# Eight filling tiles, later conditioning columns, a reordered last round with early outputs, a third raw pair, and operand sums in place

## The chip, the core and the metric

The kernel runs on one core of one Trainium2 chip. The metric is the device time of one execution, in microseconds (us). TensorE is called PE, VectorE DVE, ScalarE ACT, GpSimd POOL and SyncE SP in the profile; SP issues all of the kernel's transfers, in one queue.

## What is computed

One decoder block on 1024 tokens of width 1024, in float32. Only the second half of it is touched here:

```python
cond = silu(c) @ ada_w + ada_b            # six vectors: shift1, scale1, gate1, shift2, scale2, gate2
x = x + gate1 * (y @ w_out)               # after the token mixers
h2 = modulate(rmsnorm(x, norm2_g), shift2, scale2)
g_ff, up_ff = split(h2 @ w_ffn_in, 2)     # 1024 -> 2 x 2816
x = x + gate2 * ((silu(g_ff) * up_ff) @ w_ffn_out)
return modulate(rmsnorm(x, norm_f_g), shift_f, scale_f)
```

## The kernel before

Everything is held transposed: features on the 128 partitions, tokens along the free axis, in two halves of 512. `xs[0]` to `xs[7]` are the eight feature tiles of x (`x_76` to `x_83` in the listings). A float32 product is made from three matmuls of split operands (high times high, low times high, high times low). A split is an ACT copy to a rounded high part and a subtraction for the low part (`split`, lines 501 to 503), on DVE or POOL.

The FFN's input projection is done in 22 tiles of 128 gate and 128 up features. A tile is a two-by-two block product by Strassen and Winograd's scheme: seven products, numbered 1 to 7, instead of eight, each of 12 matmuls with 512 columns. Its weights (two raw tiles of 512 KB from `wf`) are combined on DVE into sums (`s_f`, `raw_f`) and split into `w_f_1` to `w_f_7`; the operands of h2 are combined and split once, into `h_p_5`, `h_p_6` and so on for p from 0 to 3. Bank B takes products 1, 6, 7 and 4 in turn with snapshots between, bank C 5 and 3, bank A 2.

Products 1 and 2 need only the first half of the tokens. For some tiles they are made ahead (`ahead_quad`), written to device memory (`ahead`) and read back later. `N_AHEAD` = 12 of these run beside the convolution. `N_FILL` = 4 more, f from 12 to 15, are written in the code between the second half's output projection and the FFN. The other 6 tiles are whole: all seven products inside the loop. `tile_order` spreads the whole tiles over the loop, at places 0, 4, 8, 13, 17 and 21; the partial ones have 60 matmuls, the whole ones 84.

After each pair of tiles, `finish_tile` combines the activations and writes seven operands to device memory (`acts`). It keeps its tiles in two sets of six halves of `xs`, whose own values wait in device memory (`x_mid`) meanwhile. The last 24 conditioning columns (gate2 and the final shift and scale) are a background list: `ada_cols` loads a column block into `xs[5]` or `xs[6]` and reduces it on DVE (line 143), one for each tile begun. Raw weights have four buffers (`N_RAW`), split weights eight (`N_W`).

The down projection follows in three rounds of 4, 4 and 3 pairs. Each round loads the operands, splits them (`fa`), and runs four groups n of seven products; each product is added into `xs` by a gated DVE operation (line 769). In the last round the squares of the finished tiles are summed over features by small matmuls with a vector of ones (line 801). At the end, for three pieces of the tokens (512, 256, 256), a root, a reciprocal and small matmuls (line 851) give the scale, and eight outputs a piece follow on DVE (line 855), ACT (line 857) and SP (line 858).

A scheduler that simulates the engines' times fixes the order of instructions on each engine when the kernel is built; the code's order, waits and priorities bound it. Each engine then runs its own queue in order.

Of the kernel before, what the change touches and what calls it, by code (L numbers as in the profile page):

```python
# [7 lines left out]
F32 = mybir.dt.float32  # L8
# [5 lines left out]
P = 128  # L14
S = 1024
# [18 lines left out]
N_FILL = 4  # L34
# [27 lines left out]
def block_kernel(ctx: ExitStack, tc: tile.TileContext, xT, c, ada, cols, vbias, bs, wsp,  # L62
# [442 lines left out]
    def product(bank, w_units, movs, first, cols=slice(0, H)):  # L505
        n = len(movs)
        for p, ((shi, slo), mv) in enumerate(zip(w_units, movs)):
            mhi, mlo = full(mv)
            for i, (s, m) in enumerate(((shi, mhi), (slo, mhi), (shi, mlo))):
                PE.matmul(bank[:, cols], s, m[:, cols], start=first and p == 0 and i == 0,  # L510
                          stop=p == n - 1 and i == 2, skip_group_check=True)
# [78 lines left out]
    def stationary(name, srcs, width):  # L590

        raw = []
        for i, src in enumerate(srcs):
            r = sb.tile([P, 2, width], F32, tag="raw", name=f"raw_{name}_{i}", bufs=N_RAW)
            nc.sync.dma_start(r, src)
            raw.append(r)
# [6 lines left out]
        def put(*products):  # L603
            for m in products:
# [8 lines left out]
                w = sb.tile([P, 2, H], F32R, tag="w", name=f"w_{name}_{m}", bufs=N_W)[:, :, 0:width]  # L613
# [10 lines left out]
    for p in range(4):  # L624
# [8 lines left out]
        def put(m, src):  # L633
            res[m] = moving_tile(m, f"h2_{p}_{m}")
            split(res[m], src, V)
# [13 lines left out]
    sets = [[xs[k][:, hs(half)] for k in ks for half in range(2)] for ks in ((7, 3, 2), (0, 4, 1))]  # L649
# [7 lines left out]
    def finish_tile(i, g0, g1):  # L657
# [12 lines left out]
        G.tensor_tensor(b12, g1, b12, op=ALU.subtract)  # L670
        moved(i, 7, b12)
        G.tensor_tensor(b11, b12, b11, op=ALU.add)
# [11 lines left out]

    def begin(f):
        st, put = stationary(f"f{f}", [wf[2 * f + 1].rearrange("p (a b) -> p a b", a=2),
                                       wf[2 * f].rearrange("p (a b) -> p a b", a=2)], H)
# [15 lines left out]
    for i, f in enumerate(order):  # L703
# [27 lines left out]
        if full7:  # L731
            A.activation(g0, b_bank, AF.Silu)
        else:
            V.tensor_tensor(g0, b_bank, s1, op=ALU.add)
            A.activation(g0, g0, AF.Silu)  # L735
# [10 lines left out]
    A.activation(warm, epst, AF.Sqrt)  # L746


    for k in (0, 4, 1, 5, 6, 2, 3, 7):
        nc.sync.dma_start(xs[k], x_mid[k])  # L750
    f0 = 0
    for r, pairs in enumerate(ROUNDS):
# [11 lines left out]
        st, banks = {}, {}  # L764

        def gate(bank, dests, cols=slice(0, H)):
            for k, half in dests:
                part = slice(half * H + cols.start, half * H + cols.stop)
                V.scalar_tensor_tensor(xs[k][:, part], bank[:, cols], ccol(GATE2, k),  # L769
                                       xs[k][:, part], op0=ALU.mult, op1=ALU.add)  # L770

        def step(n, m, bank, first, dests):
            product(bank, st[n][m], [v[m] for v in mov], first)
            gate(bank, dests)

        def begin_out(n):
            st[n], put = stationary(f"d{r}_{n}", [src_w[base + i].rearrange("p (a b) -> p a b", a=2)
                                                  for i in (n, n + 4)], pairs * P)
            put(1, 5, 6, 2, 7, 4, 3)
            banks[n] = mm_bank(f"B{r}_{n}")  # L780
            step(n, 1, banks[n], True, ((n, 0),))

        begin_out(0)
        for n in range(4):
            c_bank = cv_bank(f"C{r}_{n}")
            a_bank = gn_bank(f"A{r}_{n}")
            if last_round and n == 0:
                pieces = [(nrm_bank("ssq_nf0"), slice(0, H)),
                          (gn_bank("ssq_nf1"), slice(H, H + 256)),
                          (mm_bank("ssq_nf2"), slice(H + 256, S))]  # L790
                seen = [0, 0, 0]

            def square(i, k):

                bank, part = pieces[i]
                size = part.stop - part.start
                nq = size // P
                t = ev(f"sq_nf{i}_{k}")[:, 0:size]
                A.activation(t, xs[k][:, part], AF.Square)
                for q in range(nq):  # L800
                    PE.matmul(bank[q * 32:(q + 1) * 32, 0:P], ones.broadcast_to([P, 32]),  # L801
                              t[:, q * P:(q + 1) * P], start=seen[i] == 0, stop=seen[i] == KD - 1)
                seen[i] += 1

            fin = last_round and n == 3
            if not fin:
                step(n, 5, c_bank, True, ((n + 4, 1),))
            step(n, 6, banks[n], False, ((n, 1),))
            step(n, 2, a_bank, True, ((n, 0),))
            if last_round:  # L810
                square(0, n)
            if not fin:
                step(n, 7, banks[n], False, ((n + 4, 1),))
            if last_round and not fin:
                square(1, n + 4)
                square(2, n + 4)
            if n < 3:
                begin_out(n + 1)
            if fin:
                step(n, 5, c_bank, True, ((n + 4, 1),))  # L820
                step(n, 7, banks[n], False, ((n + 4, 1),))
# [112 lines left out]
```

## Time and profile before

| | |
|---|---|
| median of 3 runs | 1080.92 us (1079.58 to 1084.81) |
| profiled execution | 1082.03 us, span 1080.2 us |
| PE busy | 996.0 us, 92% |
| DVE busy | 856.5 us, 79% |
| ACT busy | 471.0 us, 44% |
| POOL busy | 379.6 us, 35% |
| data moved | 177.62 MB, mean 164 GB/s |

The span runs from the first to the last instruction. In the sliced view each digit is the busy share, in tenths, of one of 40 equal slices of 27 us; PEclk is the clock that was granted to TensorE. In a list of groups, the part after the bar gives total busy time, the mean duration in ns, and the idle time of the engine just before with what ended it. In a list of waits the three numbers are total us, times and the longest.

### The profile page before, as it was taken

The page shows a single profiled execution, that of the slowest core. Times are in us where ns is not written, and L with a number is a line of the kernel's source. Part 1 is how long each engine was busy: PE and PEld are TensorE (multiplying, and loading weights), DVE is VectorE, ACT ScalarE, POOL GpSimd, SP SyncE. Part 2 cuts the span into 40 slices and gives each one's busy share as a digit, 9 for nine tenths or more (in the row PEclk, how much of TensorE's full clock was granted, in tenths as well). Part 3 has the DMA queues.
Part 4 walks back from the last instruction along what each step waited for, and adds up shares of the span by engine and source line. Part 5 has one row for each costly group of instructions (what it writes and reads, how often), then busy time and mean ns, then how long its engine had stood idle before and what let it go on. Part 6 is the DMA issues. An engine that isn't in the chain of part 4 may idle for free. (4 is left out here: it accounts for less than half of the span.)

```text
span 1080.2 us, 13272 instructions
## 1 busy us (share of the span) xinstructions
PE 996.0 (92%) x4685; PEld 789.0 (73%) x4685; DVE 856.5 (79%) x1222; ACT 471.0 (44%) x750; POOL 379.6 (35%) x217
## 2 busy tenths in 40 slices
PE   4899999899979999977988999999899999999993
PEld 2677777578757777855866878878787788888772
DVE  5969999699899434799987777667677999969645
ACT  5248484554465433543322233323334636335326
POOL 4419894574546202231532344344243200000000
PEclk9999999999989999977999999999999999999996
DMA  9584351433435525557755445354357937414104
GB/s 335 197 269 139 124 160 48 154 118 107 146 127 180 194 85 172 199 175 250 271 190 184 146 157 194 111 183 146 116 175 273 345 133 223 166 59 137 30 1 156
DMA packets 70689, 177.62 MB, mean 164 GB/s; under 512 B 7868, under 2 KB 10172, under 8 KB 70622
## 3 DMA queue, kind: packets, MB, share of 16 engines
q1 hardware_dynamic: 70622, 176.77, 48.6%
q8 instruction: 37, 0.61, 0.2%
q14 instruction: 30, 0.25, 0.1%
HBM read 137.68 MB, written 39.06 MB: 164 GB/s over the span
## 5 line engine op out<-in xcount | busy, mean ns | idle before, releaser
L510 PE MATMUL B<-h,w_f 128*128 128x512 f32 x864 | 214.7, 402 | 16.9 <-DVE u L713 8.9
L510 PEld LDWEIGHTS B<-h,w_f 128*128 128x128 f32 x864 | 167.2, 195 | 57.6 <-DVE u L713 10.2
L448 DVE SCALAR_TENSOR_TENSOR cv<-ypad,colt,cv 128x512 f32<-128x512 f32 x216 | 150.0, 745 | 0.9
L510 PE MATMUL C<-h,w_f 128*128 128x512 f32 x528 | 132.5, 400 | 11.2 <-ACT h L502 3.8
L510 PE MATMUL B<-fa,w_d 128*128 128x512 f32 x528 | 127.5, 391 | 0.7 <-DVE fa L503 0.5
L510 PEld LDWEIGHTS C<-h,w_f 128*128 128x128 f32 x528 | 101.3, 193 | 34.7 <-ACT h L502 4.3
L510 PEld LDWEIGHTS B<-fa,w_d 128*128 128x128 f32 x528 | 98.3, 188 | 23.0 <-DVE fa L503 1.6
L502 ACT ACTIVATE w_f<-raw_f 128x512 fp32r<-128x512 f32 x100 | 61.1, 625 | 95.5 <-PE B L510 42.0
L503 DVE TENSOR_TENSOR w_f<-raw_f,w_f 128x512 fp32r<-128x512 f32 x100 | 89.2, 901 | 8.0 <-ACT w_f L502 8.0
L510 PE MATMUL ah<-h,wh_a 128*128 128x512 f32 x256 | 83.7, 405 | 5.7 <-DVE h L205 4.8
L502 ACT ACTIVATE w_d<-raw_d 128x512 fp32r<-128x512 f32 (+1 forms) x72 | 42.2, 593 | 91.0 <-PE B L510 49.1
L171 POOL TENSOR_TENSOR wl_a<-raw_a,wh_a 128x1024 fp32r<-128x1024 f32 x16 | 38.3, 2396 | 78.0 <-ACT wh_a L170 76.3
L510 PE MATMUL C<-fa,w_d 128*128 128x512 f32 (+1 forms) x273 | 65.0, 383 | 0.0
L736 POOL TENSOR_TENSOR x<-x,up 128x512 f32<-128x512 f32 x16 | 23.1, 1446 | 113.9 <-ACT x L735 113.9
L510 PEld LDWEIGHTS ah<-h,wh_a 128*128 128x128 f32 x256 | 49.1, 193 | 18.6 <-DVE h L205 6.0
L769 DVE SCALAR_TENSOR_TENSOR x<-B,cond,x 128x512 f32<-128x512 f32 x48 | 35.7, 746 | 30.2 <-PE B L510 29.7
L187 PE MATMUL p<-h,wh_vg 128*128 128x512 f32 x128 | 52.2, 414 | 7.8 <-ACT h L209 7.0
L607 DVE TENSOR_TENSOR s_f<-raw_f,raw_f 128x512 f32<-128x512 f32 x22 | 16.2, 739 | 53.5 <-DMA raw_f<-wf 53.5
L171 POOL TENSOR_TENSOR wl_vg<-raw_vg,wh_vg 128x1024 fp32r<-128x1024 f32 x16 | 44.1, 2765 | 40.3 <-ACT wh_vg L170 40.2
L510 PEld LDWEIGHTS C<-fa,w_d 128*128 128x128 f32 x273 | 50.0, 188 | 10.8 <-DVE w_d L503 0.4
L503 DVE TENSOR_TENSOR fa<-a,fa 128x512 fp32r<-128x512 f32 x77 | 53.5, 723 | 0.1
L502 ACT ACTIVATE fa<-a 128x512 fp32r<-128x512 f32 x77 | 47.0, 627 | 14.3 <-DMA a<-acts 10.4
(212 smaller groups left out, 2098.3 us busy)
## 6 DMA issues: line engine op xcount, KB each, us to landing
raw_f<-wf SPq DMA_DIRECT2D x44, 512.0 KB, 4.4
acts<-x SPq DMA_DIRECT2D x77, 256.0 KB, 4.0
a<-acts SPq DMA_DIRECT2D x77, 256.0 KB, 3.9
ada<-ada SPq DMA_DIRECT2D x24, 512.0 KB, 3.3
x<-ada SPq DMA_DIRECT2D x24, 512.0 KB, 3.6
ypad<-ada SPq DMA_DIRECT2D x16, 512.0 KB, 4.8
raw_vg<-wvg SPq DMA_DIRECT2D x16, 512.0 KB, 4.7
raw_o<-wo SPq DMA_DIRECT2D x16, 512.0 KB, 3.5
```

The lines of the kernel that those rows point to most:

```text
L171: lo_eng.tensor_tensor(lo, raw, hi.bitcast(F32), op=ALU.subtract)
L187: PE.matmul(acc, shi, mhi, start=start, stop=False)
L448: V.scalar_tensor_tensor(accs[j], src, wc, accs[j], op0=ALU.mult, op1=ALU.add)
L502: A.activation(dst[:, 0, :], src, AF.Copy)
L503: lo_eng.tensor_tensor(dst[:, 1, :], src, dst[:, 0, :].bitcast(F32), op=ALU.subtract)
L510: PE.matmul(bank[:, cols], s, m[:, cols], start=first and p == 0 and i == 0, stop=p == n - 1 and i == 2, skip_group_check=True)
L607: V.tensor_tensor(s3, a11, a21, op=ALU.subtract)
L736: G.tensor_tensor(g0, g0, up0, op=ALU.mult)
L769: V.scalar_tensor_tensor(xs[k][:, part], bank[:, cols], ccol(GATE2, k), xs[k][:, part], op0=ALU.mult, op1=ALU.add)
```

## The change

1. `N_FILL` is 8: f from 12 to 19 are made ahead, four more than before, and only two tiles are whole, at places 0 and 21.
2. The low halves of `h_p_4` and `h_p_3` are split on POOL instead of DVE.
3. The 24 conditioning columns start three tiles later (three empty entries), then come two a tile for five tiles, then one; they use `xs[5]` and `xs[1]`.
4. Every third tile's raw weights go to `xs[0]` and `xs[4]`, a third pair of buffers.
5. `finish_tile` forms its sums in the tiles that it has, so that a set has four halves instead of six.
6. The last round has an order written out by hand, with the third products of groups 1 to 3 and product 5 of group 3 last. Its squares are added on POOL before the small matmuls. Some of its split weights use buffers of the moving operands (`KEPT`). The first piece's norm and four of its outputs are issued before the last products; two of its outputs are multiplied on POOL.
7. The root's table load is tied to the last silu.

```diff
-N_FILL = 4
+N_FILL = 8
...
-            split(res[m], src, V)
+            split(res[m], src, G if m in (4, 3) else V)
...
-    sets = [[xs[k][:, hs(half)] for k in ks for half in range(2)] for ks in ((7, 3, 2), (0, 4, 1))]
+    sets = [[xs[k][:, hs(half)] for k in ks for half in range(2)] for ks in ((7, 3), (6, 2))]
...
-        t1, t4 = sets[i % 2][4:]
-        G.tensor_tensor(t1, b12, b11, op=ALU.subtract)
-        moved(i, 5, t1)
+        G.tensor_tensor(b11, b12, b11, op=ALU.subtract)
+        moved(i, 5, b11)
         G.tensor_tensor(b12, g1, b12, op=ALU.subtract)
         moved(i, 7, b12)
-        G.tensor_tensor(b11, b12, b11, op=ALU.add)
-        moved(i, 6, b11)
-        G.tensor_tensor(t4, g0, b11, op=ALU.subtract)
-        moved(i, 4, t4)
+        G.tensor_tensor(g1, g1, b11, op=ALU.subtract)
+        moved(i, 6, g1)
+        G.tensor_tensor(g0, g0, g1, op=ALU.subtract)
+        moved(i, 4, g0)
...
-    background += [lambda i=i: ada_cols(GATE2 * 8 + i, dst=xs[(5, 6)[i % 2]]) for i in range(24)]
+    background += [last_columns] * 3
+    background += [lambda i=i: last_columns(2 * i, 2 * i + 1) for i in range(5)]
+    background += [lambda i=i: last_columns(i) for i in range(10, 24)]
...
+    spare = [xs[k] for k in (0, 4)]
...
+                             spare if i % 3 == 2 and i < NF - 4 else None)
...
-    A.activation(warm, epst, AF.Sqrt)
+    with tc.issue_after(last["silu"]):
+        A.activation(warm, epst, AF.Sqrt)
...
+    with tc.issue_after(last_ins):
+        step(1, 3)
+        square(1, 1)
+        norm(0)
+        step(2, 3)
+        norm_banks[1], norm_banks[2] = gn_bank("ssq_nf1"), mm_bank("ssq_nf2")
+        square(2, 1, late=True)
+        early_sums(1)
+        step(3, 5)
+        square(7, 1, late=True)
+        output(0, (0, 1, 2, 4), by_pool=())
+        for part in pieces[1:]:
+            step(3, 3, slice(part.start - H, part.stop - H))
+            square(3, 1, part, late=True)
+    with tc.high_priority():
+        norm(1)
+        norm(2)
+    output(0, (3, 5, 6, 7), by_pool=(3, 5))
+    output(1)
+    output(2)
```

How it moves instructions is seen on POOL where the FFN's operands are prepared. Before, after the last filling tile's low half (`wl_a`, not shown), POOL forms eight operand sums (`h_12`, `h_21`) and goes on to the first tile's activations (`x_83`):

```order
L639 TENSOR_TENSOR h_12_0_3592<-h_22_0_3593,h_12_0_3592 128x512
L639 TENSOR_TENSOR h_12_1_3621<-h_22_1_3622,h_12_1_3621 128x512
L643 TENSOR_TENSOR h_21_0_3591<-h_21_0_3591,h_11_0_3590 128x512
L643 TENSOR_TENSOR h_21_1_3620<-h_21_1_3620,h_11_1_3619 128x512
L639 TENSOR_TENSOR h_12_2_3650<-h_22_2_3651,h_12_2_3650 128x512
L643 TENSOR_TENSOR h_21_2_3649<-h_21_2_3649,h_11_2_3648 128x512
L639 TENSOR_TENSOR h_12_3_3679<-h_22_3_3680,h_12_3_3679 128x512
L643 TENSOR_TENSOR h_21_3_3678<-h_21_3_3678,h_11_3_3677 128x512
L736 TENSOR_TENSOR x_83<-x_83,s_16_3816 128x512
```

After, on the same engine at the same place (the first 12 of 20 rows before its first activation):

```order
L171 TENSOR_TENSOR wl_a_3594<-raw_a_3591,wh_a_3593 128x1024
L171 TENSOR_TENSOR wl_a_3631<-raw_a_3628,wh_a_3630 128x1024
L646 TENSOR_TENSOR h_12_0_3740<-h_22_0_3741,h_12_0_3740 128x512
L646 TENSOR_TENSOR h_12_1_3769<-h_22_1_3770,h_12_1_3769 128x512
L650 TENSOR_TENSOR h_21_0_3739<-h_21_0_3739,h_11_0_3738 128x512
L171 TENSOR_TENSOR wl_a_3668<-raw_a_3665,wh_a_3667 128x1024
L503 TENSOR_TENSOR h_0_4_3761<-h_21_0_3739,h_0_4_3761 128x512
L650 TENSOR_TENSOR h_21_1_3768<-h_21_1_3768,h_11_1_3767 128x512
L171 TENSOR_TENSOR wl_a_3705<-raw_a_3702,wh_a_3704 128x1024
L503 TENSOR_TENSOR h_1_4_3790<-h_21_1_3768,h_1_4_3790 128x512
L646 TENSOR_TENSOR h_12_2_3798<-h_22_2_3799,h_12_2_3798 128x512
L650 TENSOR_TENSOR h_21_2_3797<-h_21_2_3797,h_11_2_3796 128x512
```

The four new low halves and the splits (L503) stand among the sums; in all POOL has 20 operations there instead of 8.

On DVE the same stretch ends, before, like this: the last operand splits (`h_3_7`, `h_3_6`) with conditioning columns (L143) between, 59 rows after the first scaling of h2 (L629):

```order
L143 SCALAR_TENSOR_TENSOR x_82,cond<-x_82,cact 128x1024
L612 TENSOR_TENSOR raw_f_0_3988<-raw_f_0_3988 128x512
L503 TENSOR_TENSOR h_3_7_3696<-h_12_3_3679,h_3_7_3696 128x512
L640 TENSOR_TENSOR h_11_3_3677<-h_22_3_3680,h_11_3_3677 128x512
L143 SCALAR_TENSOR_TENSOR x_81,cond<-x_81,cact 128x1024
L503 TENSOR_TENSOR w_f_4_3905<-raw_f_1_3888,w_f_4_3905 128x512
L503 TENSOR_TENSOR w_f_3_3909<-raw_f_0_3886,w_f_3_3909 128x512
L503 TENSOR_TENSOR h_3_6_3693<-h_11_3_3677,h_3_6_3693 128x512
```

After, it ends with DVE's rows 494 to 502, the last of these the second tile's fifth weight, on which TensorE's next products rest:

```order
L503 TENSOR_TENSOR h_3_6_3841<-h_11_3_3825,h_3_6_3841 128x512
L143 SCALAR_TENSOR_TENSOR x_77,cond<-x_77,cact 128x1024
L611 TENSOR_TENSOR s_f_4134<-x_76,x_80 128x512
L527 TENSOR_TENSOR ahead_3701<-ah_19_3723,ahead_3701 128x512
L616 TENSOR_TENSOR raw_f_0_4032<-raw_f_0_4032 128x512
L503 TENSOR_TENSOR w_f_3_3958<-raw_f_0_3931,w_f_3_3958 128x512
L503 TENSOR_TENSOR w_f_6_4040<-raw_f_0_4032,w_f_6_4040 128x512
L143 SCALAR_TENSOR_TENSOR x_81,cond<-x_81,cact 128x1024
L503 TENSOR_TENSOR w_f_5_4043<-raw_f_1_4034,w_f_5_4043 128x512
```

The operand splits stand 8 rows earlier, the split weights of two tiles later; up to here DVE has 59 rows in both kernels.

At the end of the program DVE has, after the change, four outputs of the first piece (`of_0` to `of_4`) ahead of the last gated additions (`x_79`); before, all outputs stood behind them:

```order
L859 SCALAR_TENSOR_TENSOR x_83<-C_3_8194,cond,x_83 128x512
L826 SCALAR_TENSOR_TENSOR of_0_8211<-x_76,cond,ssq_nf_7989 128x512
L826 SCALAR_TENSOR_TENSOR of_1_8215<-x_77,cond,ssq_nf_7989 128x512
L826 SCALAR_TENSOR_TENSOR of_2_8219<-x_78,cond,ssq_nf_7989 128x512
L826 SCALAR_TENSOR_TENSOR of_4_8223<-x_80,cond,ssq_nf_7989 128x512
L859 SCALAR_TENSOR_TENSOR x_79<-C_3_8194,cond,x_79 128x256 x2
L808 RECIPROCAL rt_nf_8255<-rt_nf_8255 64x128
```

The first piece's reciprocal has moved ahead of these rows as well.

More of the change, by code (lines that the diff above doesn't have):

```diff
@@ new lines, in square @@
+    def square(k, half, cols=None, late=False):
+        part = cols or (slice(0, H) if half == 0 else slice(H, S))
+        t = ev(f"sq_nf{half}_{k}_{part.start}")[:, 0:part.stop - part.start]
+        A.activation(t, xs[k][:, part], AF.Square)
+        if not late:
+            if half not in sums:
+                sums[half] = t
+            else:
+                G.tensor_tensor(sums[half], sums[half], t, op=ALU.add)
+            return
+        for i, p in enumerate(pieces):
+            if p.start >= part.start and p.stop <= part.stop:
+                to_partitions(i, t[:, p.start - part.start:p.stop - part.start])
@@ L763, in block_kernel @@
         base = 0 if last_round else 8 * r
[L764 to L774, printed above, removed]
+        st, b_banks, c_banks = {}, {}, {}
```

189 lines of the change are left out of this document (106 added, 83 removed).

## The prediction

> **What bounds the kernel now.** The page comes first: TensorE is busy for 92% of the span.
>
> ```profile
> span 1080.2 us, 13272 instructions
> PE 996.0 (92%) x4685; PEld 789.0 (73%) x4685; DVE 856.5 (79%) x1222; ACT 471.0 (44%) x750; POOL 379.6 (35%) x217
> PE   4899999899979999977988999999899999999993
> PEclk9999999999989999977999999999999999999996
> ```
>
> The slices put the holes that this change can reach at slices 17 to 21 (the start of the FFN) and at the last one. Program order does not change before TensorE's 458.3 us. So I asked for the stretches from there on, of line L510 (all products) alone, then of all engines:
>
> ```profile
> 458.30:499.40 41.10, 27.33 (x78) 18.20 (x77) 0.68 0.52 175
> 499.40:839.40 340.00, 325.21 (x1402) 265.97 (x1401) 0.98 0.55 186
> 839.40:1055.60 216.20, 210.46 (x922) 170.59 (x921) 1.00 0.40 133
> ...
> 458.30:499.40 41.10, 27.33 (x78) 18.20 (x77) 41.10 (x61) 17.05 (x29) 11.36 (x6) 0.68 0.52 175
> 1055.60:1080.20 24.60, 6.43 (x48) 4.77 (x48) 14.89 (x28) 15.32 (x31) 0.00 (x0) 0.59 0.49 172
> ```
>
> Columns: length, busy us and count by engine, granted clock, DMA share, GB/s. At full rate a product costs 0.227 us, read from the chain:
>
> ```profile
> 880.45 5.44 PE B L510 x24
> ```
>
> So the transition loses 41.1 - 78 x 0.227 = 23.4 us, the FFN loop 340.0 - 1402 x 0.227 = 22 us, the down-projection rounds about 5, and 24.6 us pass after the last product. In the transition VectorE (DVE) is busy all 41.10 us: it bounds. In the loop TensorE waits for it too, and DVE waits for weights:
>
> ```profile
> PE B L510 <- DVE u L713: 8.9, 3, 4.1
> PE B L510 <- DVE x L713: 3.0, 1, 3.0
> ...
> DVE s_f L607 <- DMA raw_f<-wf: 53.5, 16, 6.3
> ...
> 699.57 2.88 PE L510 MATMUL A<-h,w_f 128*128 128x512 f32 x12
> 713.26 0.69 DVE L607 TENSOR_TENSOR s_f<-raw_f,raw_f 128x512 f32<-128x512 f32 x1 [5.13 <-DMA raw_f<-wf]
> 715.33 0.96 PE L510 MATMUL B<-h,w_f 128*128 128x512 f32 x3 [2.00 <-DVE u L713]
> ```
>
> DVE's queue is in order: a weight sum that waits 5.13 us for its load holds back the snapshot (L713) behind it, and TensorE then waits 2.00. This stands behind a whole tile (seven products; only those have an A), whose seven split weights free the raw buffers late.
>
> **The filling tiles.** Each of the four new ones is 24 products, 5.44 us, taken out of a later tile: TensorE's work is unchanged, 96 x 0.227 = 21.8 us of it moves into the hole. Fill and the ten C products between end at 458.3 + 106 x 0.227 = 482.4 us; another 24 products (B, A) at 487.8. Then TensorE's next rows need the split weights of the second tile, DVE's row 502 (w_f_5_4043), so I count DVE.
>
> ```profile
> 443.00:499.40 56.40, 42.63 (x150) 30.98 (x149) 56.40 (x83) 27.05 (x46) 14.60 (x8) 0.77 0.56 189
> 446.72 1.05 PE L238 MATMUL ssq_n<-rt_n,colt 128*128 128x128 f32 x8
> 449.41 1.40 DVE L629 SCALAR_TENSOR_TENSOR h<-x,cond,ssq_n 128x512 f32<-128x512 f32 x2
> 495.74 0.68 DVE L503 TENSOR_TENSOR h<-h,h 128x512 fp32r<-128x512 f32 x1
> 496.34 1.21 DVE L143 SCALAR_TENSOR_TENSOR x<-x,cact 128x1024 f32<-128x1024 f32 x1
> L143 DVE SCALAR_TENSOR_TENSOR x<-x,cact 128x1024 f32<-128x1024 f32 x9 | 10.9, 1211 | 0.0
> ```
>
> Before, from 449.41 to the last sixth-operand split, begun at 495.74, DVE runs 59 instructions: 8 scalings (two in 1.40 us, 0.66 apart), 7 conditioning columns (1.21), 44 others (0.60 from start to start, as 495.74 and 496.34). Undisturbed that is 5.3 + 8.5 + 26.4 = 40.2 us; it took 47.0, to 496.42. The 6.8 us are collisions with POOL:
>
> ```profile
> 626.10 1.61 POOL L670 TENSOR_TENSOR x<-x,x 128x512 f32<-128x512 f32 x1
> 626.50 1.77 DVE L503 TENSOR_TENSOR w_f<-raw_f,w_f 128x512 fp32r<-128x512 f32 x1
> 627.79 1.62 POOL L672 TENSOR_TENSOR x<-x 128x512 f32<-128x512 f32 x1
> 628.19 0.68 DVE L723 TENSOR_TENSOR s<-A,s 128x512 f32<-128x512 f32 x1
> ```
>
> A DVE operation with both inputs in SBUF, begun while POOL works, takes 1.77 instead of 0.68 us; one that reads PSUM (A) does not. With 8 POOL operations this was 6.8 / 8 = 0.85 us each. After, rows 444 to 502 hold the same mix of 59, can start at 447.8 (when L238 ends), but up to 20 POOL operations fall beside them: four low halves of 128x1024, eight operand sums and eight splits moved from DVE. At 0.85, and 0.8 more for two long ones: 447.8 + 40.2 + 17 + 1.6 = 507, or 505 as a few POOL splits slip behind. The bounds are 488 (no collision) and 522 (each POOL operation costs its whole 1.7 us). I take 505, near the measured 0.85. TensorE then stands some 17 us, but has done 132 products at 505, against 78 at 499.4: 54 x 0.227 - 5.6 = 6.7 us won. The extra loads, writes and reads (512 KB and four of 256 KB a tile) lie beside a DMA share of 0.52 to 0.55 and cost nothing; without that cover, one late landing costs about the 4.4 us of a raw load.
>
> By the Trainium skill's "SBUF — State Buffer" (SBUF: two separate sides) the ports that VectorE and GpSimd share are an exclusive lock held for the whole instruction, so the loser stands still throughout; that speaks against moving splits to POOL. The sum by it is the 522 us end; the rows, 0.85 us per operation, are nearer half.
>
> **The loop.** 1332 products remain: 505 + 302.4 = 807 us with no loss. The adas still to run are 17, delayed but not fewer: two a tile on DVE.
>
> ```profile
> 540.00:822.00 282.00, 267.67 (x1154) 219.13 (x1153) 204.76 (x261) 83.39 (x145) 113.55 (x72) 0.98 0.49 163
> L143 DVE SCALAR_TENSOR_TENSOR x<-x,cact 128x1024 f32<-128x1024 f32 x5 | 7.2, 1434 | 4.0 <-DMA x<-ada 4.0
> ```
>
> (204.8 - 7.2) / 17.6 tiles = 11.2 us of DVE per tile, collisions in it, against 60 x 0.227 = 13.6 us of TensorE for a partial tile. Both kinds of tile issue 14 DVE operations, so 20 partial tiles leave DVE 2.4 us of slack each. The 17 columns at 1.43 us are 24 us; six tiles' slack covers 14. Being ahead by a tile's weights covers part of the rest: 5 us lost here (0 to 10). After that, no whole tile follows but the last, and a third pair of raw buffers lets loads go a tile earlier: of the 8.9 us of L713 waits I leave 2. Cold products after the stalls: 2. The FFN ends at 807 + 9 = 816, where before it was 839.4 less 12 products of the next round already done, 836.7: 20.7 us won, of which I take 20. Sums in place remain four POOL operations a pair; two now wait for a write to be read out, 4 us, on an engine idle for 65% of the span, so nothing; if POOL had no slack, eleven pairs times 4 us would be due.
>
> **Rounds and tail.** Rounds 0 and 1 are the same code: nothing (either way 2 us). The kept weights are the same splits into other buffers, covered by a TensorE that never waited for them in the rounds; without that cover one split, 0.7 us, would show. In the last one, 64 small squares' products become 28, and nine POOL additions replace the rest:
>
> ```profile
> L801 PE MATMUL ssq_nf<-sq_nf,ones 128*32 128x128 f32 x128 | 7.4, 280 | 0.6 <-ACT sq_nf L799 0.6
> 1041.13 1.50 PE L801 MATMUL ssq_nf<-sq_nf,ones 128*32 128x128 f32 x32
> 1060.41 3.23 PE L851 MATMUL ssq_nf<-rt_nf,colt 128*128 128x128 f32 x12 [2.25 <-DVE rt_nf L849]
> ```
>
> At 1.44 us in 32 passes, 96 of 128 stand ahead of the last product before, 48 after: 2.1 us less, given back by the first norm's 8 passes of L851, 2.1 us, which now stand there. One POOL addition (1.6 us) between a square and its product can hold TensorE 1 us: +1. After the last product:
>
> ```profile
> 1057.71 1.28 ACT L848 ACT_TABLE_LOAD   x1
> 1062.53 6.14 DVE L855 SCALAR_TENSOR_TENSOR of<-x,cond,ssq_nf 128x512 f32<-128x512 f32 x10 [1.36 <-PE ssq_nf L851]
> 1069.45 5.47 DVE L855 SCALAR_TENSOR_TENSOR of<-x,cond,ssq_nf 128x256 f32<-128x256 f32 x14
> 1064.12 13.60 SPq L858 DMA_DIRECT2D out<-of  x24
> ```
>
> The square-root table load goes ahead (-1.3); four of eight wide outputs (0.75 us each) run before the last products and two go to POOL (-4.5); the first norm's chain (reciprocal 0.9, L851 2.1, its semaphores) is already done (-3). Against this, the last gates queue behind four outputs on DVE (+0.8). Together -8: the tail would be 16.6 us. Bounds: -5 if the 20 remaining output issues, 13.60 / 24 = 0.57 us each, set the pace; -10 if not even the gates wait.
>
> **Sum.** -20 + 0 + 1 - 8 = -27 us against the profiled execution's 1082.03 us (span 1080.2), 1055; the median of the runs shown, 1080.92, is 1.1 lower: about 1054.
>
> **Rivals.** (a) Each POOL operation costs DVE its whole length where they stand dense: TensorE resumes at 522, and the columns meet a DVE that is later still, 10 us lost instead of 5. FFN end 816 + 17 + 5 = 838, tail -8: 1075, on the median's scale as all of these. For it: the 1.77 us row; against: PSUM readers pass, and the measured mean is half of that. 0.10. This is the SBUF page's lock taken literally; the trace agrees with it for single operations, not for the mean.
> (b) Collisions hide in DVE waits, since POOL's own inputs come from DVE: TensorE resumes at 493, loop loss 6: FFN end 801, tail -9: 1037 to 1042. For it: POOL waited 21.4 and 20.5 us for DVE in its two transition lines. 0.25.
>
> ```profile
> L643 POOL TENSOR_TENSOR h<-h,h 128x512 f32<-128x512 f32 x4 | 8.8, 2198 | 20.5 <-issue 12.1 <-DVE h L640 8.4
> L639 POOL TENSOR_TENSOR h<-h,h 128x512 f32<-128x512 f32 x4 | 5.8, 1451 | 21.8 <-DVE h L637 21.4 <-ACT h L630 0.4
> ```
>
> (c) The third pair does not do what it says: every raw load still stands in the one SP queue behind activation writes that wait for POOL, so the loop keeps its 22 us. FFN end 505 + 302 + 22 = 829: 1066. For it: 53.5 us of DVE waiting for loads; against: those waits went with the whole tiles. 0.12.
> (d) Slower: the partial tiles make DVE the bound.
>
> ```profile
> raw_f<-wf SPq DMA_DIRECT2D x44, 512.0 KB, 4.4
> ```
>
> 20 of them come in a row with no whole tile of 84 x 0.227 = 19 us to catch up in; if each waits out one raw load, DVE needs 11.2 + 4.4 = 15.6 us a tile against 13.6, and 20 tiles lose 40 us: FFN end 505 + 302 + 40 = 847, and 1084 with the shorter tail. It decides above 15.4 us a tile, where the FFN's loss (37 us) eats the tail's gain. Against: in the loop DVE stood idle for 27% of the time, the waits for loads in it. 0.05.
>
> **Numbers.** The forecast as summed (1044 to 1062) has 0.45, (b) 0.25, (c) 0.12, (a) 0.10, (d) 0.05, and 0.03 is for a mixture that comes out even. The range from 1038 to 1070 leaves out (a), (d), the even mixture and the lowest of (b), 0.2 together. About 0.5% (5.4 us) is what a measurement of this kernel can tell from no change; (a) lies just beyond that, so I count 0.08 of it as faster, 0.02 as the same: faster 0.90, same 0.05, slower 0.05.
>
> **What would show it.** The transition: no hole at 458.3, TensorE at full rate to about 485, then a hole until 505; wrong if it resumes before 495 or after 515. The loop: no L713-type waits after the last column; DVE's waits for raw loads well under 53.5 us. Collisions: the mean of DVE's splits in the transition above 0.85 us. Tail: 16 to 18 us after the last product, no table load in it, DVE idle before the first reciprocal. The prediction fails most easily on how much POOL's 20 operations cost DVE, which no stretch of before shows at that density.

## The result

The changed kernel takes 1054.06 us (median of four runs, 1051.26 to 1055.96) against 1082.87 for the kernel before on the same chip: ratio 0.9737, 95% interval 0.9706 to 0.9769. A second set of runs gave 1053.93. The profiled execution took 1055.96, its span is 1053.9 us, 26.3 shorter than before's 1080.2.

The page of the changed kernel:

```profile
span 1053.9 us, 13171 instructions
PE 983.6 (93%) x4613; PEld 783.7 (74%) x4613; DVE 868.5 (82%) x1216; ACT 466.4 (44%) x732; POOL 413.2 (39%) x240
PE   4899999889979999979898999999999999999994
PEclk9999999999989999989898999999999999999998
```

The share of busy time says little (92% became 93%); the slices say more. Counted from 0, the dent at slices 17 to 21 is shallower and falls apart into three single slices, 17, 19 and 21. By stages, first the products alone (L510), then all engines of the tail:

```profile
458.30:505.00 46.70, 38.77 (x154) 30.38 (x153) 0.89 0.59 205
505.00:820.00 315.00, 305.81 (x1318) 250.21 (x1317) 0.98 0.61 209
822.07:1038.10 216.03, 208.91 (x922) 171.17 (x920) 1.00 0.40 134
...
1038.10:1053.90 15.80, 2.24 (x17) 1.32 (x16) 10.05 (x21) 10.63 (x24) 2.49 (x2) 0.67 0.63 217
```

Read as the prediction read its own: the transition up to 505 loses 46.7 - 154 x 0.227 = 11.7 us; the loop from there 315.0 - 1318 x 0.227 = 15.8; the three rounds take 216.0 us for the same 922 products that took 216.2; the tail is 15.8 us instead of 24.6. The FFN's last product, with the 12 products of the next round that run ahead of it taken off, ends at 819.4 instead of 836.7. That makes -17.4 in the FFN, 0 in the rounds and -8.8 in the tail, which is the 26.3 of the spans.

TensorE's longest waits from 455 us on, and DVE's wait for raw weights:

```profile
PE ah L510 <- DVE ahead L527: 6.3, 1, 6.3
PE B L510 <- DVE w_f L503: 4.6, 2, 3.5
PE B L510 <- DVE x L729: 4.0, 1, 4.0
...
DVE s_f L611 <- DMA raw_f<-wf: 4.1, 2, 2.3
```

The 53.5 us that DVE waited for raw loads have gone. The first row is a wait that the prediction did not have. The timeline of TensorE, DVE and POOL around it:

```profile
464.05 0.39 PE L510 MATMUL ah<-h,wh_a 128*128 128x512 f32 x1
470.75 0.79 PE L510 MATMUL ah<-h,wh_a 128*128 128x512 f32 x1 [6.31 <-DVE ahead L527]
...
459.88 2.88 DVE L611 TENSOR_TENSOR s_f<-raw_f,raw_f 128x512 f32<-128x512 f32 x1
467.26 2.83 DVE L612 TENSOR_TENSOR raw_f<-raw_f 128x512 f32<-128x512 f32 x1
470.02 0.68 DVE L527 TENSOR_TENSOR ahead<-ah,ahead 128x512 f32<-128x512 f32 x1
...
459.38 2.84 POOL L171 TENSOR_TENSOR wl_a<-raw_a,wh_a 128x1024 fp32r<-128x1024 f32 x1
466.75 2.79 POOL L171 TENSOR_TENSOR wl_a<-raw_a,wh_a 128x1024 fp32r<-128x1024 f32 x1
```

A filling tile needs two banks of PSUM (the memory that the products are summed up in), out of three that take turns, and DVE's sum (L527) frees the second. The sum stands in DVE's queue behind operations that POOL stretched, among them two weight sums that went from 0.68 to 2.88 and 2.83 us beside long POOL operations. TensorE has the first product of the sixth filling tile next in its program (72 products of filling tiles are left at that point, six groups of 12), and this takes the bank of the fourth one's second product. Until the fourth tile's sum ends, at 470.70, that bank is not free, and TensorE stands still.

Further on, TensorE's rows at the place where the prediction had a hole of 17 us, and the two longest stalls after it:

```profile
499.88 3.01 PE L510 MATMUL B<-h,w_f 128*128 128x512 f32 x12
504.00 2.79 PE L510 MATMUL B<-h,w_f 128*128 128x512 f32 x11 [1.10 <-DVE w_f L503]
515.77 10.33 PE L510 MATMUL B<-h,w_f 128*128 128x512 f32 x33 [3.54 <-DVE w_f L503]
563.86 5.86 PE L510 MATMUL B<-h,w_f 128*128 128x512 f32 x14 [4.00 <-DVE x L729]
```

Each is the first row after its wait. In the last two the products also run slower: 33 take 10.33 us, where 33 x 0.227 = 7.5. The tail:

```profile
1033.67 2.72 DVE L826 SCALAR_TENSOR_TENSOR of<-x,cond,ssq_nf 128x512 f32<-128x512 f32 x4 [1.33 <-PE ssq_nf L810]
1036.84 1.33 PE L510 MATMUL C<-fa,w_d 128*128 128x256 f32 x9 [1.58 <-DVE x L859]
1041.93 6.67 DVE L826 SCALAR_TENSOR_TENSOR of<-x,cond,ssq_nf 128x256 f32<-128x256 f32 x16
1043.72 7.81 SPq L829 DMA_DIRECT2D out<-of  x16
```

Four wide outputs run beside the last product, whose second half waits 1.58 us for a gate behind them. Four wide outputs, two of them on POOL, and 16 narrow ones remain, and the queue that issues the narrow ones is busy until 1051.5, 2.4 us before the span's end.

### The profile page after: what moved, and what is told of

It is laid out like the page before. It is cut to its first block, busy times and chain, and to the rows that moved or that the text cites. A ratio compares the mean times of both kernels' runs of the same rounds, so it can differ in the third digit from the quotient of the medians.

```text
span 1053.9 us, 13171 instructions
## 1 busy us (share of the span) xinstructions
PE 983.6 (93%) x4613; PEld 783.7 (74%) x4613; DVE 868.5 (82%) x1216; ACT 466.4 (44%) x732; POOL 413.2 (39%) x240
## 4 chain that ended last, share of the span: by engine, by line
PE 68%; DVE 19%; DMA 4%; issue 4%; ACT 3%; POOL 1%; SPq 0%; ACTq 0%; DVEq 0%; POOLq 0%
PE B L510 23%; PE C L510 13%; PE ah L510 6%; DVE x L143 3%; PE po L187 3%; PE A L510 3%; PE po L188 3%; PE po L189 3%; DVE w_f L503 2%; PE v L187 2%; PE v L188 1%; PE v L189 1%; PE pu L188 1%; PE p L189 1%; PE pu L189 1%
## 5 line engine op out<-in xcount | busy, mean ns | idle before, releaser
L510 PE MATMUL B<-h,w_f 128*128 128x512 f32 x816 | 199.0, 397 | 9.3 <-DVE w_f L503 4.6
L510 PEld LDWEIGHTS B<-h,w_f 128*128 128x128 f32 x816 | 156.4, 192 | 44.5 <-DVE w_f L503 5.4
L510 PE MATMUL B<-fa,w_d 128*128 128x512 f32 x528 | 126.8, 390 | 2.8 <-DVE x L859 1.7
L510 PE MATMUL C<-h,w_f 128*128 128x512 f32 x528 | 127.7, 390 | 0.6 <-DVE u L754 0.5
L510 PEld LDWEIGHTS B<-fa,w_d 128*128 128x128 f32 x528 | 98.6, 188 | 25.2 <-DVE x L859 2.5
L510 PE MATMUL ah<-h,wh_a 128*128 128x512 f32 x320 | 106.0, 409 | 11.9 <-DVE ahead L527 6.6
L510 PEld LDWEIGHTS C<-h,w_f 128*128 128x128 f32 x528 | 98.9, 188 | 22.2 <-issue 1.4
L510 PEld LDWEIGHTS ah<-h,wh_a 128*128 128x128 f32 x320 | 62.5, 197 | 28.3 <-DVE ahead L527 7.3
L791 POOL TENSOR_TENSOR sq_nf<-sq_nf,sq_nf 128x512 f32<-128x512 f32 x9 | 12.0, 1345 | 181.9 <-ACT sq_nf L786 181.8
L171 POOL TENSOR_TENSOR wl_a<-raw_a,wh_a 128x1024 fp32r<-128x1024 f32 x20 | 48.7, 2439 | 85.9 <-ACT wh_a L170 84.0
L503 DVE TENSOR_TENSOR w_f<-raw_f,w_f 128x512 fp32r<-128x512 f32 x68 | 68.1, 1012 | 5.9 <-ACT w_f L502 5.9
L502 ACT ACTIVATE w_f<-raw_f 128x512 fp32r<-128x512 f32 x68 | 41.6, 625 | 58.6 <-PE B L510 23.9
L510 PE MATMUL C<-fa,w_d 128*128 128x512 f32 (+1 forms) x273 | 64.9, 384 | 1.6 <-DVE x L859 1.6
L510 PE MATMUL ah<-h,wl_a 128*128 128x512 f32 x160 | 65.6, 410 | 0.0
L187 PE MATMUL p<-h,wh_vg 128*128 128x512 f32 x128 | 52.4, 416 | 7.4 <-ACT h L209 6.7
L510 PEld LDWEIGHTS C<-fa,w_d 128*128 128x128 f32 x273 | 50.0, 188 | 12.3 <-DVE x L859 1.8
L189 PE MATMUL p<-h,wh_vg 128*128 128x512 f32 x128 | 49.8, 409 | 3.6 <-DVE h L210 3.6
L503 DVE TENSOR_TENSOR fa<-a,fa 128x512 fp32r<-128x512 f32 x77 | 52.3, 708 | 0.1
```

Source lines behind the costliest of these rows:

```text
L171: lo_eng.tensor_tensor(lo, raw, hi.bitcast(F32), op=ALU.subtract)
L187: PE.matmul(acc, shi, mhi, start=start, stop=False)
L189: PE.matmul(acc, shi, mlo, start=False, stop=stop)
L502: A.activation(dst[:, 0, :], src, AF.Copy)
L503: lo_eng.tensor_tensor(dst[:, 1, :], src, dst[:, 0, :].bitcast(F32), op=ALU.subtract)
L510: last_mm = PE.matmul(bank[:, cols], s, m[:, cols], start=first and p == 0 and i == 0, stop=p == n - 1 and i == 2, skip_group_check=True)
```

## The experiments

Each kernel is the changed one with one edit, unless said otherwise; all were timed beside the kernel before, whose median was 1082.2 to 1082.9 in every set. The scheduler works out the order of instructions anew for each kernel, so an edit can also move instructions that it does not name.

**Four filling tiles.**

```diff
-N_FILL = 8
+N_FILL = 4
```

> Four filling tiles instead of eight; all else as in the changed kernel. Theory A (the filling tiles carry the gain of the transition): at 505 us the changed kernel has done 153 products against about 103 before, 50 x 0.227 = 11.4 us; without the four tiles that is lost again, and some 3 us more, because six whole tiles again hold raw buffers long: 1054 + 14 = 1066 to 1070, with a hole of over 15 us between 458 and 505. Theory B (the third raw pair and the operand sums in place carry it, the fill only moves the wait): within 3 us of 1054, and TensorE's holes after 505 shorter by as much as those before are longer.

Measured: 1066.85 us (ratio to before 0.9849, 0.9827 to 0.9872), 12.8 more than the changed kernel. Its products:

```profile
458.30:505.00 46.70, 26.18 (x79) 16.94 (x77) 0.75 0.53 167
505.00:820.00 315.00, 309.81 (x1354) 254.41 (x1355) 0.99 0.55 186
```

Theory A. Without the four tiles 75 fewer products are done at 505 us, 17 us of TensorE; but the loop behind it, with six whole tiles in it, loses only 315.0 - 1354 x 0.227 = 7.6 us instead of 15.8. So beside this kernel the fill wins 17 us and gives 8 back. That is 9 of the 10.9 us between the two profiled executions (the medians are 12.8 apart); the rest is not placed.

**No third raw pair.**

```diff
-                             spare if i % 3 == 2 and i < NF - 4 else None)
+                             None)
```

> No third raw pair: all weight loads in the four raw buffers as before; all else as in the changed kernel. Theory A (the third pair took the waits for raw loads away): DVE's waits for raw loads rise from 4.1 us to over 25, TensorE waits for DVE's snapshots again, and the time is 1059 to 1062. Theory B (the waits stood behind whole tiles and went with them, the third pair does nothing): DVE's raw waits stay under 12 us, and the time is 1054 plus or minus 1.5.

Measured: 1063.92 us (0.9836, 0.9812 to 0.9860), 9.9 more. DVE's waits and TensorE's:

```profile
DVE s_f L611 <- DMA raw_f<-wf: 32.7, 15, 3.2
...
PE B L510 <- DVE x L729: 9.5, 6, 6.1
...
546.40 7.64 PE L510 MATMUL B<-h,w_f 128*128 128x512 f32 x21 [6.08 <-DVE x L729]
...
590.00:800.00 210.00, 204.07 (x891) 165.95 (x890) 1.00 0.52 171
```

Theory A for a part of it. 15 loads are late again, the first of them at 578 us. From 590 to 800 us, where no column is left, TensorE is busy 204.07 us instead of 209.54 in the changed kernel, and waits four times some 0.8 us for a snapshot (L729) and up to 1.39 us for the sum L754. These waits do not stand behind whole tiles alone. But the longest wait, 6.08 us, comes before any load is late; it is a wait for a snapshot queued behind columns and collisions, as the one of 4.00 us at 563.9 in the changed kernel. And at 505 us only 137 products are done, against 154: DVE runs the transition in another order here, with a column of 2.31 us at 454.9 that the changed kernel does not have there. So some 5.5 us of the 9.9 are shown to be the third pair's work in the loop. The rest lies before 590 us; that the other order costs it is likely, but not shown.

**Both at once**, four filling tiles and no third pair:

> Four filling tiles and no third raw pair together; what stays of the change is the tail, the later columns, the splits on POOL and the sums in place. Theory A (the two parts stand apart, one in the transition, the other in the loop): their costs add, 1054 + 12.8 + 9.9 = 1076 to 1078; the kernel before with the new tail would be 1082.5 - 7.8 = 1074.7, so what stays in the FFN would be worth nothing or cost 2 us. Theory B (the third pair is needed because twenty partial tiles stand in a row and the loads come sooner; behind six whole tiles two pairs are nearly enough): 1067 to 1071, and what stays in the FFN would be worth some 5 us.

Measured: 1078.89 us (0.9971, 0.9952 to 0.9991), 24.9 more than the changed kernel. The parts cost 12.8 and 9.9 alone, 22.7 in sum: within 2.2 us they add, as theory A has it, though 1078.89 is 0.9 above its range. The other edits of the FFN are then worth 1074.7 - 1078.9, some 4 us of loss, by subtraction. Where that lies the transitions show: the kernel before, then this one, products first, all engines behind them, in a fence each.

```profile
458.30:505.00 46.70, 32.93 (x100) 22.80 (x99) 0.71 0.58 201
...
443.00:505.00 62.00, 48.23 (x172) 35.58 (x171) 60.91 (x90) 29.98 (x50) 14.60 (x8) 0.78 0.60 207
```

```profile
458.30:505.00 46.70, 27.54 (x75) 17.87 (x74) 0.71 0.55 178
...
443.00:505.00 62.00, 42.84 (x146) 30.69 (x145) 61.40 (x78) 26.67 (x46) 27.33 (x16) 0.78 0.63 204
```

With the same four filling tiles 25 fewer products are done at 505 us, 5.7 us of TensorE; POOL is busy 27.33 us instead of 14.60, with 16 operations for 8, and DVE, busy throughout, does 78 instead of 90 instructions, 8 of the difference being the splits it gave away. The splits on POOL are the edit that fits this; they were not tried alone with four filling tiles.

**The rounds and the tail of before**, behind the changed FFN:

> The changed kernel's FFN with the rounds and the tail of the kernel before (the square root of the epsilon, which loads the table, stays where the change put it, behind the last Silu). Theory A (the tail's 8.8 us come from early outputs, POOL's outputs and the early first norm): 1054 + 9 = 1062 to 1065, with some 24 us after the last product. Theory B (after the last product the 24 output issues, 13.6 us on their queue, set the pace in both, so most of the shorter tail is paid for by products that end later): 1054 to 1058.

Measured: 1061.81 us (0.9809, 0.9787 to 0.9832), 7.8 more. Theory A, 0.2 us under its range: 21.7 us pass after the last product instead of 15.8. They are not the 24.6 of the kernel before, in part because the table load of 1.28 us stays where the change put it. The second norm of this kernel and its output queue:

```profile
1049.18 1.22 PE L868 MATMUL ssq_nf<-rt_nf,colt 64*128 64x128 f32 x4 [6.45 <-DVE rt_nf L866]
...
1043.72 13.03 SPq L875 DMA_DIRECT2D out<-of  x24
```

Here one norm waits 6.45 us behind ten outputs in DVE's queue, and 24 issues take 13.03 us behind the last product; in the changed kernel the last 16 take 7.81, and all 20 behind that product 10.3.

**Columns spread over the loop.** Each column is queued on DVE behind a sum of an earlier tile:

```diff
-            ada_cols(GATE2 * 8 + i, dst=xs[(5, 1)[i % 2]])
+            with tc.issue_after(last["tile_sum"]):
+                ada_cols(GATE2 * 8 + i, dst=xs[(5, 1)[i % 2]])
...
-    background += [lambda i=i: last_columns(2 * i, 2 * i + 1) for i in range(5)]
-    background += [lambda i=i: last_columns(i) for i in range(10, 24)]
+    background += [lambda i=i: last_columns(i) for i in range(12)]
+    background += [lambda i=i: last_columns(2 * i, 2 * i + 1) for i in range(6, 12)]
...
-        V.tensor_tensor(u2, c_bank, u2, op=ALU.add)
+        last["tile_sum"] = V.tensor_tensor(u2, c_bank, u2, op=ALU.add).ins
```

> The 24 last conditioning columns are held back behind the C sum of the tile two earlier, one a tile from the third tile on and two a tile for the last six; all else as in the changed kernel. Theory A (the 3.5 us wait at 515.8 and the 4.0 us wait at 563.9, with about 3 us of cold products behind them, come from columns that stand dense on DVE): both waits go, nothing takes their place, 1054 - 9 = 1044 to 1048. Theory B (DVE is short of time all through the loop, 11.2 us a tile of 13.6 without a column, so a column costs TensorE the same wherever it stands): 1052 to 1056.

Measured: 1057.77 us (0.9771, 0.9749 to 0.9793), no gain, and rather 3.7 lost. I had expected theory A. Products and the largest wait:

```profile
458.30:505.00 46.70, 40.80 (x169) 33.23 (x169) 0.93 0.41 144
505.00:820.00 315.00, 300.70 (x1286) 243.05 (x1285) 0.98 0.64 212
...
PE B L510 <- DVE x L730: 8.0, 7, 2.3
PE B L510 <- DVE u L730: 3.2, 1, 3.2
```

The transition gains 15 products, the loop loses 32. The wait at 563.9 has gone. That at 515.8 has not quite: one of 3.23 us stands at 511.7, for a snapshot (L730, the old L729) for which DVE itself waits 3.73 us, until a product made ahead is read back. And seven waits for snapshots came up further on, the longer ones, of 1.42 to 2.34 us, from 710 us on, where two columns a tile stand. A tile's 11.2 us on DVE and two columns of 1.2 make 13.6, all of TensorE's time for a tile: behind a late load there is nothing to catch up with.

**Columns from the first tile on**, instead of the fourth:

> The 24 last conditioning columns come one a tile from the first tile on instead of from the fourth; all else as in the changed kernel. Theory A (columns in the transition cost DVE's time at the place that bounds): the three that come sooner cost 3 x 1.21 = 3.6 us, 1057 to 1059. Theory B (the instruction order hardly changes, the first column of the last 24 standing at DVE's row 456 instead of 466, and what is delayed in one place is made up in the other): 1053 to 1055.5.

Measured: 1057.14 us (0.9764, 0.9735 to 0.9793), 3.1 more than the changed kernel, at theory A's number; but the interval meets that of the changed kernel, and B is not excluded. At 505 us 142 products are done instead of 154, 2.7 us of TensorE, which speaks for A: the loss lies in the transition. A's reason for it, the columns' own time on DVE, cannot be told there from the other order of DVE's instructions that came with the edit.

**Another bank for the filling tiles.**

```diff
-            bank = mm_bank(f"ah{m}_{f}")
+            bank = (gn_bank if m == 1 and f >= N_AHEAD else mm_bank)(f"ah{m}_{f}")
```

> The second product of each of the eight filling tiles takes a bank of another PSUM pool, so it need not wait for DVE's sum of the filling tile two earlier; all else as in the changed kernel. Theory A (the 6.3 us hole at 464.4 is a wait for a free bank, and TensorE's time there is lost for good): the hole and some 2 us of cold products behind it go, 1046 to 1049. Theory B (DVE's row of the second tile's split weights, at 505 us, ends the fill whatever TensorE does before it, so the hole only moves behind the fill): TensorE waits there instead, 1053 to 1056.

With this the second products take turns in two banks of another pool. These are freed by the same sums, so the wait does not go, as had been expected: it only comes one product of 12, 2.7 us, later.

Measured: 1057.62 us (0.9771, 0.9744 to 0.9797). Not faster, and I had expected theory A here too. TensorE's rows after its waits:

```profile
469.33 0.50 PE L510 MATMUL ah<-h,wh_a 128*128 128x512 f32 x1 [2.60 <-DVE ahead L527]
485.06 0.80 PE L510 MATMUL ah<-h,wh_a 128*128 128x512 f32 x1 [4.51 <-DVE ahead L527]
505.82 4.24 PE L510 MATMUL B<-h,w_f 128*128 128x512 f32 x11 [2.51 <-DVE w_f L503]
```

The hole of 6.31 us became one of 2.60, for the same tile's sum, and one of 4.51, for the sum of the filling tile two later, and there is more waiting at 505. What was given at one place was lost at the next, to a DVE that was late at each. A bank that does not wait for DVE at all was not tried.

**The eight splits back on DVE.**

```diff
-            split(res[m], src, G if m in (4, 3) else V)
+            split(res[m], src, V)
```

> The eight splits of the operands 4 and 3 go back from POOL to DVE; all else as in the changed kernel. Theory A (a POOL operation costs DVE 0.87 us beside it, an own split 0.60): DVE is 8 x 0.27 = 2.2 us earlier at the second tile's weights, 1052 to 1055, no measurable difference. Theory B (a POOL operation costs DVE its whole 1.7 us, the lock of the SBUF page of the Trainium skill taken literally): 8.8 us earlier, 1045 to 1048. Theory C (most collisions are hidden in DVE's waits, so the move to POOL was a gain of 8 x 0.60 = 4.8 us): 1058 to 1060.

Measured: 1052.48 us (0.9724, 0.9693 to 0.9755): no difference that this measurement can tell, at the lower end of theory A's. At 505 us 158 products are done, against 154. So POOL's help is worth nothing that could be measured here, and its operations do not cost DVE their whole length: theories B and C fall.

**Two early outputs instead of four.**

```diff
-        output(0, (0, 1, 2, 4), by_pool=())
+        output(0, (0, 1), by_pool=())
...
-    output(0, (3, 5, 6, 7), by_pool=(3, 5))
+    output(0, (2, 4, 3, 5, 6, 7), by_pool=(3, 5))
```

> Two early outputs (tiles 0 and 1) instead of four ahead of the last gates; tiles 2 and 4 come behind the last products. Theory A (the 1.58 us that the last half of the last product waits for a gate behind four outputs is time of the end): the wait goes, two outputs of 0.67 us come back behind it on a DVE that waits for the norms there: 1052.5 to 1053.5. Theory B (behind the last product the outputs set the pace one by one, so every output taken back costs its own time): 1054 to 1056.

Measured: 1052.88 us (0.9727, 0.9700 to 0.9754), inside A's numbers, but no difference beyond the runs' spread. The wait of 1.58 us shrinks to 0.26, while the time behind the last product grows from 15.8 to 17.0.

**Sixteen columns in the rounds.** After the other bank and the spread columns one theory was left for what TensorE still loses between 458 and 590 us: DVE has too much to do there, and only work that leaves the stretch helps. The columns of the last norm aren't needed before the outputs:

```diff
-    background += [lambda i=i: last_columns(2 * i, 2 * i + 1) for i in range(5)]
-    background += [lambda i=i: last_columns(i) for i in range(10, 24)]
+    background += [lambda i=i: last_columns(i) for i in range(8)]
...
+        if r == 1:
+            background += [lambda i=i: ada_cols(GATE2 * 8 + 8 + 2 * i, 2) for i in range(4)]
+            background += [lambda i=i: ada_cols(GATE2 * 8 + 16 + 4 * i, 4) for i in range(2)]
```

The finishing of these two groups moves behind the last round's products with them.

> Of the 24 last conditioning columns, only the eight that the gates need stay in the FFN; the sixteen of the last norm stand in the second and third down-projection round, where DVE is busy 58.8 of 72 and 52.0 of 73 us; all else as in the changed kernel. Theory A (what TensorE still loses between 458 and 590 us, some 20 us, is lost to a DVE short of time, and columns are the part of its work that can stand elsewhere): sixteen columns of 1.2 to 1.4 us leave, 10 to 14 us won, 1040 to 1045, with no new wait over 1 us in the rounds. Theory B (the loss is that of order, as when the banks or the columns were moved: each hole is followed by another): 1051 to 1057. Theory C (the columns' loads take the raw buffers of the rounds' weights): TensorE waits for split weights there, 1055 to 1065.

> The same sixteen columns in the rounds, and besides the eight splits back on DVE and two early outputs instead of four. Theory A: the two small gains (1.6 and 1.2 us, each within what the runs vary) add to the columns': 1038 to 1043. Theory B (DVE, no longer short of time where the splits return, needed POOL's help less, or the splits cost what they relieve): no different from the columns alone, plus or minus 2.

> The changed kernel itself, unchanged, beside the two above on one chip: 1052 to 1056 by every theory; it gives the difference to them without the spread between chips.

Measured on one chip: the changed kernel 1053.93 us (0.9723, 0.9694 to 0.9752), sixteen columns in the rounds 1045.13 (0.9639, 0.9613 to 0.9664), with splits and outputs besides 1042.00 (0.9617, 0.9588 to 0.9646). All engines from 505 to 590 us, of these three in that order, in a fence each:

```profile
505.00:590.00 85.00, 76.76 (x313) 61.41 (x312) 83.57 (x116) 24.01 (x40) 29.94 (x19) 0.92 0.74 254
```

```profile
505.00:590.00 85.00, 83.18 (x360) 68.29 (x359) 75.65 (x97) 29.20 (x48) 32.86 (x21) 0.98 0.55 186
...
893.00:965.00 72.00, 12.27 (x20) 1.00 0.60 197
965.00:1030.00 65.00, 4.89 (x8) 1.00 0.21 70
```

```profile
505.00:590.00 85.00, 85.00 (x376) 70.41 (x375) 76.93 (x99) 28.95 (x47) 38.33 (x23) 1.00 0.57 197
```

DVE falls from 83.57 to 75.65 us busy in these 85, and TensorE does 360 products instead of 313; in the last kernel it never stops. The two rows in the middle fence are the columns (L143) in the rounds: 17 us of DVE there, and the only new wait of TensorE over 1 us in them is one of 1.3, for split weights. Of the waits of 3.54 and 4.00 us the first shrinks to 1.82 and the second goes. Theory A; its gain of 10 to 14 us was set too high, 8.8 came. The eight columns that stay also come one a tile here instead of two, which was not tried by itself. The last kernel is the fastest of the study, 11.9 us under the changed one; that the splits and outputs add anything to the columns isn't certain, since the ranges of the two kernels overlap (1042.5 to 1046.5 and 1039.3 to 1044.8).

## Why the prediction was right, and where it was not

The forecast was about 1054 us; the sum -27 stands against -26.3 in the spans. Its parts did worse than its total: that the total came so close is luck, as errors of opposite sign met in the FFN.

**The transition: wrong in how it runs.** "No hole at 458.3, then a hole until 505" was the reverse of what came. DVE was forecast exactly: its row 502, put at 505, is this one, and ends at 505.69.

```profile
505.01 0.68 DVE L503 TENSOR_TENSOR w_f<-raw_f,w_f 128x512 fp32r<-128x512 f32 x1
```

The step that failed is "then TensorE's next rows need" that row. In TensorE's order two more groups stand ahead of the product that uses it: 12 products with the first tile's sixth weight, which need DVE's row 494, and 11 with the second tile's sixth weight, which need row 500. They ran from 499.88 to 506.6, and TensorE lost 1.10 us there, not 17. But these 23 products account for only 5.2 us of the 17. Most of the rest was lost earlier, at what the forecast had missed on the other side, the PSUM bank: 6.31 us at 464.4, and nearly 3 after it at half rate, since 14 products took 6.13 us. Without that loss TensorE would have come some 9 us sooner to the rows that need 494 and 500, and stood there. At 505 us 154 products were done instead of 132 (the forecast's own 106 and 24 make 130; before: 100): 5 us better than forecast.

**The collisions: right.** From 448.1 to 505.7 DVE needed 57.6 us for the rows put at 40.2 without collisions; 1.7 of that is waiting, so some 18 POOL operations cost 15.7 us, 0.87 each (forecast 0.85). Taken row by row, 15 of the 59 are stretched, by 15.8 us together, and the mean of the splits (L503) was 1.02 us, above the 0.85 that was set as the sign. With the splits back on DVE, the time did not move measurably, as this price says. By the Trainium skill's "SBUF — State Buffer" (SBUF: two separate sides) the lock holds throughout an operation. The row that went from 0.68 to 2.88 us beside a POOL operation of 2.84 agrees with it for one collision. But the POOL operation of 2.41 us at 448.2 stretched none of the four scalings beside it, and on the mean the cost is about half of an operation's 1.8 us. So rival (a), which charged the whole length each time, fell.

**The loop: mechanism right, two terms too small.** Forecast loss 9 us, measured 15.8. The waits behind columns were 3.54 and 4.00, 7.5 for the 5 set down; without most of the columns 1.82 of them stayed. The cold products were put at 2 and came to 5.5: 10.33 - 33 x 0.227 = 2.8 behind the one, 5.86 - 14 x 0.227 = 2.7 behind the other. The waits behind raw loads, set at 2, did not come: DVE's two late loads cost TensorE nothing. The rest is 0.9 for the next round's operands (three waits for `fa`), 0.5 for the sum L754 behind a DVE that POOL had stretched, and small gaps. The 1.10 at 504 belongs to the transition. The part of the term that was called slack failed worst: "six tiles' slack covers 14" holds for a DVE that is on time, but it comes out of the transition late, and columns and catching up want the same slack. The sixteen columns of the last experiment brought 8.8 us, where the 17 still to run had been priced at 5 together.

**The third pair: right in kind.** The forecast gave it most of the 8.9 us of snapshot waits, 6.9. Taken away alone it costs 9.9, but only some 5.5 of that stands in the loop behind late loads. Rival (c) falls, and so does (d): DVE's 11.2 us per tile came out as forecast, 173.0 us in 210 with no column among them, and TensorE was busy 209.5 of those 210.

```profile
590.00:800.00 210.00, 209.54 (x925) 173.21 (x924) 172.96 (x212) 64.96 (x108) 97.83 (x63) 1.00 0.53 182
```

**Rounds and tail: right.** 0 where +1 was given, -8.8 where -8 was; the tail is 15.8 us for 16.6 forecast, with no table load in it, and the one wait that was foreseen, gates behind outputs, came (1.58 against 0.8). Undone together, but for the table load, they cost 7.8; what each part of them brings is not shown. (The prediction's "about 5" for what the rounds lose is 216.2 - 922 x 0.227 = 6.9 by its own rows; nothing hangs on it.)

The FFN's -17.4 for -20 is thus the sum of two errors of opposite sign, +5 in the transition and -7 to -8 in the loop. Rival (b) ran the transition better than forecast, as came, but put it down to hidden collisions, which did not come: POOL's operations cost what they were priced at.

What stays open is the price of the splits on POOL: neither gain nor loss with eight filling tiles, where TensorE has products to do meanwhile, and with four, by the transition's 5.7 us, probably a loss. The later columns rather gain 3, in the order of instructions that came with them. The sums in place could not be undone by themselves, since the third pair's buffers are those that they free.

## To carry to other kernels

Where an in-order engine bounds a stretch, a bank that is needed a little later, or another place for some of its work in the same stretch, moved TensorE's hole here and did not close it. What helped was work that left the stretch for one in which that engine had time to spare. Before a row of one engine is called the end of another's hole, count in the order what stands ahead of the product that needs it. And price a stall of over 3 us at its length and some 2 to 3 us of slow products behind it; stalls of 1.8 to 3 us brought up to 2 us of them here, or none.

## What had not been expected of the hardware

TensorE's clock can fall after short waits. The granted clock (the number behind the bracketed counts) of three stretches of the changed kernel, behind waits of 6.31, 3.54 and 1.72 us:

```profile
470.70:476.50 5.80, 5.75 (x14) 4.49 (x15) 0.50 0.74 260
515.80:520.00 4.20, 4.20 (x10) 3.33 (x11) 0.50 1.00 399
837.80:840.80 3.00, 3.00 (x13) 2.50 (x14) 1.00 0.73 213
```

and of the kernel with sixteen columns in the rounds, behind a wait of 1.82 us:

```profile
514.20:518.40 4.20, 4.20 (x13) 3.30 (x14) 0.65 1.00 368
```

A wait of 3.54 or 6.31 us is followed by 4 to 6 us at half clock, one of 1.82 by a part of that, one of 1.72 by none. The length alone does not decide it: in the kernel before, a wait of 2.85 us is followed by full clock.

```profile
778.31 0.96 PE L510 MATMUL B<-h,w_f 128*128 128x512 f32 x3 [2.85 <-DVE u L713]
778.31:782.31 4.00, 4.00 (x17) 3.30 (x18) 1.00 0.01 2
```

By the Trainium skill's "TensorE: Matmul & The Clock Gate" (Part 1: The HAM clock gate) the clock falls after an idle window of about 3.4 us. The half clock behind the waits of 3.54 and 6.31 us agrees with that; the one behind 1.82 us does not. What decides between the shorter waits is not shown here.
